# A matrix is loaded in squares of 32 by 32 and turned by VectorE, instead of in rows and turned by TensorE

## The chip, the cores and the metric

The kernel runs on one core of one Trainium2 chip. The metric is the device time of one execution in microseconds (us). The kernel before was timed in three runs: the median is 1117.33 us, the lowest 1117.31, the highest 1117.41. The profile comes from one more execution, taken by the hardware profiler.

A core has five engines that run side by side, each with its own queue of instructions that it takes strictly in order: TensorE (PE in the profile, with its weight loads shown apart as PEld), VectorE (DVE), ScalarE (ACT), GpSimd (POOL) and SyncE (SP). SP, ACT and POOL can also issue DMA transfers. PE reads SBUF and writes PSUM.

## The reference, cut to what matters

The network has two layers of feed-forward block, mixer, cross attention and a second feed-forward block, on 256 tokens of width 1024. The change concerns only `mem`, the memory of 256 rows and 1024 columns that cross attention reads:

```
def cross_attn(x, mem, wq, wk, wv, wo):
    ...
    q = (x @ wq).reshape(bsz, s, CA_HEADS, CA_HEAD_DIM)
    k = (mem @ wk).reshape(bsz, m, CA_HEADS, CA_HEAD_DIM)
    v = (mem @ wv).reshape(bsz, m, CA_HEADS, CA_HEAD_DIM)
```

The products with `ca_k` and `ca_v` contract over the 1024 columns of `mem`. PE contracts over partitions, so the kernel needs `mem` turned: columns on partitions, tokens along the row. The turned memory is made once and used by both layers.

## The kernel before, in words

Everything is float32, and a product is made from rounded parts: `split` (lines 60 to 62) takes a tile, lets ACT round it into a high part (line 61) and lets DVE subtract that from the source, which gives the low part (line 62). A product is then three matmuls, high by high, high by low and low by high (`mm_rows`, lines 127 to 130), all recorded on line 103.

Weights stream from HBM through `load` (lines 64 to 91). SP issues DMAs of 1 MB into a ring of three `raw` tiles (line 75); ACT and DVE split each into `whi` and `wlo` tiles, eight of each. SP therefore runs ahead of PE by as many buffers as the rings hold.

A feed-forward block (`ffn`, line 349) works in chunks of 512 hidden columns, numbered c. For each chunk `hidden` (line 440) makes the gate products and then the up products with `mm_cols`; each group of matmuls fills one PSUM tile `acc`, of which there are four, and ACT and DVE empty it (lines 123 and 124) into a tile `sg` or `up`. Tiles of the tag `up` have two buffers. After the hidden columns of chunk c, `both` multiplies earlier chunks with the down weights into PSUM tiles `dn`.

The memory enters in the first feed-forward block of layer 0. At chunk 1, `early` (lines 497 to 499) calls `load_memory` and `small_parameters`. `load_memory` (lines 174 to 183) issues two DMAs on SP, one for each half of the tokens (line 177), behind the last weight load issued so far. At chunk 2, after `hidden` and ahead of `both` (lines 500 to 502), the functions that both returned are called. The one of the memory transposes in sixteen blocks of 128 by 128: `transposed` and `transposed_half` (lines 164 to 172) let PE transpose four blocks into an `acc` tile (line 167), and `split` empties it into `mT`, the turned memory's high and low part. The one of the parameters transposes one tile `rows` (line 236). The first reader of `mT` is `keys` (line 522), after the first feed-forward block.

`small_parameters` (lines 196 to 259) also fills POOL's queue at the start: six DMAs (lines 198 to 205) and 28 mask operations on a tile `mf` (lines 215 and 219), ended by a conversion into `masks` (line 223). After that POOL has only short powers for the normalisations and a few clearing operations.

The order on each engine is set by an automatic scheduler. It takes instructions in the order of the program as their priority, and puts a later one into a gap where it finds its inputs ready. `tc.issue_after(x)` adds that what its block traces on the engine of x comes behind x in that engine's queue. The first matmuls of the kernel (line 391) and the mixer have orders written out by hand, in which the memory has no part.

Of the kernel before, what the change touches and what calls it, by code (L numbers as in the profile page):

```python
# [8 lines left out]
F32 = mybir.dt.float32  # L9
# [8 lines left out]
P = 128  # L18
DEPTH = 2
SEQ = 256  # L20
DM = 1024
DFF = 2816
NT = SEQ // P
# [23 lines left out]
def model(ctx: ExitStack, tc: tile.TileContext, t: dict, out: bass.AP):  # L47
    nc = tc.nc
# [5 lines left out]
    def acc(shape=(P, 2, SEQ), tag="acc"):  # L54
        return ps.tile(list(shape), F32, tag=tag, name=tag)
# [4 lines left out]
    def split(hi, lo, src):  # L60
        nc.scalar.copy(hi, src)  # L61
        nc.vector.tensor_tensor(lo, src, hi.bitcast(F32), op=ALU.subtract)  # L62
# [69 lines left out]
    def tok(i):  # L132
        return slice(i * P, (i + 1) * P)
# [26 lines left out]
    mTh, mTl = mT[:, :, 0, :], mT[:, :, 1, :]  # L160
# [3 lines left out]
    def transposed_half(src, i, j, dh, dl, unit=idn):  # L164
        pt = acc((P, 4, P))
        for k in range(4):
            nc.tensor.transpose(pt[:, k, :], src[:, (4 * j + k) * P : (4 * j + k + 1) * P], unit)  # L167
        split(dh[:, 4 * j : 4 * j + 4, tok(i)], dl[:, 4 * j : 4 * j + 4, tok(i)], pt)

    def transposed(src, i, dh, dl, unit=idn):  # L170
        for j in range(2):
            transposed_half(src, i, j, dh, dl, unit)

    def load_memory(mp):
        m = [mp.tile([P, DM], F32, tag="m", name="m", bufs=2) for _ in range(NT)]
        for i in range(NT):
            nc.sync.dma_start(m[i], t["mem"][0, tok(i), :])

        def later():
            for i in range(NT):  # L180
                transposed(m[i], i, mTh, mTl)

        return later

# [3 lines left out]
    masks = cst.tile([P, 1024], U8, name="masks")[:, 0 : NT * len(LEVELS) * 64].rearrange(  # L188
        "p (b n c) -> p b n c", b=NT, c=64
    )  # L190
# [5 lines left out]
    def small_parameters(op):  # L196
        nc.gpsimd.memset(rows, 0.0)
        nc.gpsimd.dma_start(rows[0:12, :], t["conv_w"].rearrange("l k (j p) -> (l k j) p", p=P))
        nc.gpsimd.dma_start(rows[12:20, :], t["rec_lb"].rearrange("l (h p) -> (l h) p", p=P))
        nc.gpsimd.dma_start(rows[20:28, :], t["rec_norm_g"].rearrange("l (h p) -> (l h) p", p=P))  # L200
        nc.gpsimd.dma_start(rows[28:32, :], t["pool_scale"].rearrange("l (j p) -> (l j) p", p=P))
        nc.gpsimd.memset(wpool, 0.0)
        for g in range(2):
            q = slice(g * 64, g * 64 + 64)
            nc.gpsimd.dma_start(
                wpool[q, :, :, q].rearrange("r l j c -> r (l j) c"),
                t["pool_w"].rearrange("l (j g) r c -> g r (l j) c", g=2)[g],
            )

        mf = op.tile([P, NT, len(LEVELS), 64], F32, name="mf", bufs=1)  # L210
        nc.gpsimd.memset(mf, 1.0)
        for b in range(NT):
            for n, c in enumerate(LEVELS):
                m = mf[:, b, n, :].rearrange("p (a c) -> p a c", c=c)
                nc.gpsimd.affine_select(
                    out=m, in_=m, compare_op=ALU.is_ge, fill=0.0, base=-b * c,
                    pattern=[[-2 * c, 64 // c], [0, c]], channel_multiplier=1,
                )
                nc.gpsimd.affine_select(
                    out=m, in_=m, compare_op=ALU.is_ge, fill=0.0, base=(1 + b) * c - 1,  # L220
                    pattern=[[2 * c, 64 // c], [0, c]], channel_multiplier=-1,
                )
        nc.gpsimd.tensor_copy(masks, mf)

        cnt = op.tile([P, 2, PAD], F32, name="cnt", bufs=1)
        wcol = op.tile([P, 2], F32, name="wcol", bufs=1)
        for g, w in enumerate(WINDOWS):
            nc.gpsimd.memset(wcol[(g % 2) * 64 : (g % 2) * 64 + 64, g // 2 : g // 2 + 1], float(w))
        nc.gpsimd.iota(
            cnt, pattern=[[0, 2], [1, PAD]], base=1, channel_multiplier=0,  # L230
            allow_small_or_imprecise_dtypes=True,
        )

        def later():
            pt = acc((P, P))
            nc.tensor.transpose(pt, rows, idn)
            nc.vector.tensor_copy(prm, pt[:, 0:32])
            for j in range(2):
                nc.vector.tensor_scalar_min(cnt[:, j, :], cnt[:, j, :], wcol[:, j : j + 1])
            nc.vector.reciprocal(invc, cnt)  # L240

            lb = [prm[:, 12:16], prm[:, 16:20]]
            mx = op.tile([P, HEADS], F32, name="mx", bufs=1)
            nc.vector.tensor_tensor(mx, lb[0], lb[1], op=ALU.max)
            e = op.tile([P, DEPTH, HEADS], F32, name="e", bufs=1)
            s = op.tile([P, HEADS], F32, name="s", bufs=1)
            for l in range(DEPTH):
                nc.vector.tensor_tensor(e[:, l, :], lb[l], mx, op=ALU.subtract)
            nc.scalar.activation(e, e, AF.Exp)
            nc.vector.tensor_tensor(s, e[:, 0, :], e[:, 1, :], op=ALU.add)  # L250
            nc.vector.reciprocal(s, s)
            for l in range(DEPTH):
                nc.vector.tensor_tensor(e[:, l, :], e[:, l, :], s, op=ALU.mult)
            nc.vector.tensor_tensor(lbs[:, 0, :], e[:, 0, :], e[:, 0, :], op=ALU.subtract)
            nc.vector.tensor_tensor(s, e[:, 0, :], e[:, 1, :], op=ALU.add)
            nc.vector.tensor_tensor(lbs[:, 1, :], s, e[:, 0, :], op=ALU.subtract)
            nc.vector.tensor_scalar(oml, lbs, -1.0, 1.0, op0=ALU.mult, op1=ALU.add)

        return later


    def ln_params(l, n):
# [259 lines left out]
    def keys(l, c, between={}):  # L522
        w = load(t["ca_k"][l], 0, NK, c * CHUNK, CHUNK)
        for p in range(2):
            o = sm.tile([P, 2, SEQ], F32, tag="sums", name="sums", bufs=1)
            for j in range(2):
                between.get(4 * p + 2 * j, lambda: None)()
                add(o[:, j, :], mm_cols(w, slice((2 * p + j) * P, (2 * p + j + 1) * P), mT))
            d = slice(4 * c + 2 * p, 4 * c + 2 * p + 2)
            split(kTh[:, d, :], kTl[:, d, :], o)  # L530
# [341 lines left out]
            return project_back([slab(a) for a in (0, 2, 4, 6)], 3, gb, 1.0)  # L872


    pend = None
    for l in range(DEPTH):
        pend = ffn(l, "ffn1", 0, pend, early=None if l else lambda op: (load_memory(op), small_parameters(op)))
        keys(l, 0, {6: pend})
        pend = mixer(l, lambda: keys(l, 1))
        pend = attention(l, pend)  # L880
        pend = ffn(l, "ffn2", 3, pend, last=l == DEPTH - 1)
# [27 lines left out]
```

## Time and profile before

| | |
|---|---|
| median of three runs | 1117.33 us |
| the profiled execution | 1118.65 us |
| its span, first to last instruction | 1116.9 us |
| PE matmuls, busy | 1102.9 us (99%), 6227 instructions |
| PE weight loads, busy | 992.6 us (89%) |
| DVE, busy | 822.4 us (74%) |
| ACT, busy | 594.2 us (53%) |
| POOL, busy | 41.8 us (4%) |
| granted TensorE clock, mean | 0.998 |
| DMA, mean over the span | 195 GB/s |

A row of the timeline gives the start of a group of like instructions in us from the span's start, the time from the first's start to the last's end, the engine, the line, the operation, the tile written and the tiles read, and how many there were; a bracket tells how long the engine had been idle before, and what ended that. Matmuls are pipelined, so the end of one lies behind the start of the next: the pace of PE is read from starts, not from durations. A row of waits gives who waited for whom, the total, how often, and the longest. Weight loads run a little ahead of their matmuls.

### The profile page before, as it was taken

The numbers are of one execution on the slowest core, as the hardware profiler recorded it, in microseconds if no ns is written. First come the engines' busy times: TensorE is split into PE (matmuls) and PEld (weight loads), VectorE is DVE, ScalarE is ACT, GpSimd is POOL, SyncE is SP. The second block draws the span as 40 slices with busy tenths as digits, with TensorE's granted clock in tenths as the row PEclk, the third lists the DMA queues.
The fourth block names the chain that finished last, engine by engine and source line by source line (L and its number), as shares of the span: only waits on it lengthen the run. The fifth ranks groups of instructions, "written<-read, shape, count | busy, mean of one in ns | idle before, by whom it ended". The sixth has DMA issues, their size and how long they took to land. (4 is left out here: it accounts for less than half of the span.)

```text
span 1116.9 us, 15747 instructions
## 1 busy us (share of the span) xinstructions
PE 1102.9 (99%) x6227; PEld 992.6 (89%) x6227; DVE 822.4 (74%) x1195; ACT 594.2 (53%) x873; POOL 41.8 (4%) x80
## 2 busy tenths in 40 slices
PE   9999999999999999999999999999999999999997
PEld 7989998998889889999889999889988998999996
DVE  6766677898888666666677666598988777766665
ACT  6665553645466456455355555455454653665550
POOL 7000000000000000000000000000000000000000
PEclk9999999999999999999999999999999999999999
DMA  8855565743465375656466655655445645755551
GB/s 309 301 211 202 194 221 156 240 170 139 163 243 180 105 262 191 226 204 211 151 226 234 214 182 186 237 186 194 151 146 183 237 152 164 249 189 203 181 182 38
DMA packets 98378, 218.23 MB, mean 195 GB/s; under 512 B 3776, under 2 KB 16352, under 8 KB 98304
## 3 DMA queue, kind: packets, MB, share of 16 engines
q1 hardware_dynamic: 97536, 215.89, 56.1%
q8 instruction: 49, 0.80, 0.3%
q10 hardware_dynamic: 576, 1.18, 0.3%
q14 instruction: 25, 0.20, 0.1%
q0 software_dynamic: 192, 0.15, 0.0%
HBM read 216.15 MB, written 1.05 MB: 194 GB/s over the span
## 5 line engine op out<-in xcount | busy, mean ns | idle before, releaser
L62 DVE TENSOR_TENSOR wlo<-raw,whi 128x1024 fp32r<-128x1024 f32 (+1 forms) x396 | 469.1, 1208 | 102.6 <-ACT whi L61 66.6
L61 ACT CAST whi<-raw 128x1024 fp32r<-128x1024 f32 (+1 forms) x396 | 398.2, 1041 | 170.7 <-PE dn L103 127.6
L103 PE MATMUL acc<-xT,whi 128*128 128x512 f32 x1600 | 388.3, 381 | 0.6 <-DVE xT L62 0.6
L103 PEld LDWEIGHTS acc<-xT,whi 128*128 128x128 f32 x1600 | 288.9, 190 | 33.8 <-DVE xT L62 1.1
L103 PEld LDWEIGHTS acc<-xT,wlo 128*128 128x128 f32 x1600 | 209.7, 191 | 10.8
L103 PE MATMUL acc<-xT,wlo 128*128 128x256 f32 x1600 | 210.8, 275 | 0.0
L103 PE MATMUL dn<-whi,ah 128*128 128x512 f32 x346 | 131.6, 380 | 0.0
L103 PE MATMUL dn<-wlo,ah 128*128 128x512 f32 x346 | 131.1, 379 | 0.0
L103 PE MATMUL dn<-whi,al 128*128 128x512 f32 x346 | 131.1, 379 | 0.0
L103 PE MATMUL dn<-whi,xT 128*128 128x512 f32 x288 | 88.9, 384 | 0.0
L103 PE MATMUL acc<-whi,xT 128*128 128x512 f32 x288 | 88.4, 381 | 0.0
L124 DVE TENSOR_TENSOR sg<-acc,sg 128x256 f32<-128x256 f32 x72 | 30.4, 422 | 69.7 <-ACT sg L123 69.6
L103 PEld LDWEIGHTS dn<-whi,al 128*128 128x128 f32 x346 | 65.4, 189 | 9.3
L103 PEld LDWEIGHTS dn<-wlo,ah 128*128 128x128 f32 x346 | 65.4, 189 | 9.2
L103 PEld LDWEIGHTS dn<-whi,ah 128*128 128x128 f32 x346 | 65.5, 189 | 8.6
L123 ACT COPY sg<-acc 128x256 f32<-128x256 f32 x72 | 26.7, 371 | 84.0 <-PE acc L103 83.8
L103 PEld LDWEIGHTS dn<-whi,xT 128*128 128x128 f32 x288 | 54.8, 191 | 7.5
L103 PEld LDWEIGHTS acc<-whi,xT 128*128 128x128 f32 x288 | 54.3, 189 | 7.6
L103 PE MATMUL dn<-wlo,xT 128*128 128x512 f32 x144 | 54.9, 381 | 0.0
L103 PE MATMUL acc<-wlo,xT 128*128 128x512 f32 x144 | 54.6, 379 | 0.0
L123 ACT COPY up<-acc 128x256 f32<-128x256 f32 x72 | 26.7, 370 | 49.0 <-PE acc L103 48.0
L304 POOL TENSOR_TENSOR rs<-rs,nhalf 128x1 f32<-128x1 f32 x16 | 14.9, 933 | 903.6 <-DVE rs L303 903.6
(196 smaller groups left out, 1048.5 us busy)
## 6 DMA issues: line engine op xcount, KB each, us to landing
raw<-in_ffn_up_dram SPq DMA_DIRECT2D x44, 1024.0 KB, 5.1
raw<-in_ffn_down_dram SPq DMA_DIRECT2D x44, 1024.0 KB, 4.9
raw<-in_ffn_gate_dram SPq DMA_DIRECT2D x42, 1024.0 KB, 5.0
raw<-in_w_in_dram SPq DMA_DIRECT2D x24, 1024.0 KB, 5.1
raw<-in_ca_k_dram SPq DMA_DIRECT2D x8, 1024.0 KB, 5.0
raw<-in_w_out_dram SPq DMA_DIRECT2D x8, 1024.0 KB, 4.9
raw<-in_ca_v_dram SPq DMA_DIRECT2D x8, 1024.0 KB, 6.0
raw<-in_ca_q_dram SPq DMA_DIRECT2D x8, 1024.0 KB, 5.0
```

The costliest lines, as they stand in the source:

```text
L61: nc.scalar.copy(hi, src)
L62: nc.vector.tensor_tensor(lo, src, hi.bitcast(F32), op=ALU.subtract)
L103: nc.tensor.matmul(o, w, x, start=start, stop=stop)
L123: nc.scalar.copy(dst, o[:, 1])
L124: nc.vector.tensor_tensor(dst, o[:, 0], dst, op=ALU.add)
L304: nc.gpsimd.tensor_tensor(rs, rs, nhalf[:, 0:1], op=ALU.pow)
```

## The change

`mem` is loaded by 32 DMAs issued on POOL, in place of two on SP. Each moves, for one strip of 32 columns, all 256 tokens into 32 partitions: the partition is the token's place within its group of 32, and along the row lie the eight groups with 32 columns each. So a tile holds squares of 32 by 32, each where it will be wanted, but each not yet turned; a run of consecutive bytes is 32 floats, 128 bytes. The DMAs are put behind the conversion to `masks` in POOL's queue. At chunk 2 four DVE transposes of 128 by 512 turn the squares, each into a tile of the tag `up`, and four `split`s write `mT` from there. The two functions at chunk 2 now come in the other order, the parameters first. PE's sixteen transposes and their four `acc` tiles are gone; the number and the size of the `split`s are the same.

```diff
-    def load_memory(mp):
-        m = [mp.tile([P, DM], F32, tag="m", name="m", bufs=2) for _ in range(NT)]
-        for i in range(NT):
-            nc.sync.dma_start(m[i], t["mem"][0, tok(i), :])
+    def load_memory(mp, behind):
+        m = [mp.tile([P, 4, 8, 32], F32, tag="m", name="m", bufs=2) for _ in range(2)]
+        with tc.issue_after(behind.ins):
+            for n in range(2):
+                for a in range(4):
+                    for k in range(4):
+                        c = (4 * n + k) * P + a * 32
+                        nc.gpsimd.dma_start(
+                            m[n][a * 32 : a * 32 + 32, k],
+                            t["mem"][0, :, c : c + 32].rearrange("(b i) j -> i b j", i=32),
+                        )
 
         def later():
-            for i in range(NT):
-                transposed(m[i], i, mTh, mTl)
+            for n in range(2):
+                for k in range(0, 4, 2):
+                    turned = mp.tile([P, 2, SEQ], F32, tag="up", name="turned")
+                    nc.vector.transpose(
+                        turned.rearrange("p k t -> p (k t)"), m[n][:, k : k + 2].rearrange("p k b j -> p (k b j)")
+                    )
+                    d = slice(4 * n + k, 4 * n + k + 2)
+                    split(mTh[:, d, :], mTl[:, d, :], turned)
...
-        nc.gpsimd.tensor_copy(masks, mf)
+        made = nc.gpsimd.tensor_copy(masks, mf)
...
-        return later
+        return later, made
...
+    def beginnings(op):
+        parameters, made = small_parameters(op)
+        return parameters, load_memory(op, made)
+
     pend = None
     for l in range(DEPTH):
-        pend = ffn(l, "ffn1", 0, pend, early=None if l else lambda op: (load_memory(op), small_parameters(op)))
+        pend = ffn(l, "ffn1", 0, pend, early=None if l else beginnings)
```

## The prediction

> **What bounds the kernel.** I read the page's busy times first, then the waits of PE and its weight loads, then the timeline of PE around the transposes that go.
>
> ```profile
> span 1116.9 us, 15747 instructions
> PE 1102.9 (99%) x6227; PEld 992.6 (89%) x6227; DVE 822.4 (74%) x1195; ACT 594.2 (53%) x873; POOL 41.8 (4%) x80
> ```
>
> PE has 14 us without work in the whole span. In the waits of the first 120 us, nothing behind the first 9 us stops PE or its weight loads but the two idle times at the memory's and the parameters' transposes. So PE sets the end here, and what leaves its queue comes off the time, unless something takes its place. The stage in question, by its timeline:
>
> ```profile
> 78.38 0.38 PE L103 MATMUL acc<-xT,whi 128*128 128x512 f32 x1
> 78.59 1.47 PE L167 MATMUL acc<-idn,m 128*128 128x128 f32 x12
> 79.82 0.46 PE L103 MATMUL dn<-whi,ah 128*128 128x512 f32 x1
> 80.12 0.38 PE L103 MATMUL dn<-wlo,ah 128*128 128x512 f32 x1
> 80.34 0.38 PE L103 MATMUL dn<-whi,al 128*128 128x512 f32 x1
> 80.71 0.66 PE L167 MATMUL acc<-idn,m 128*128 128x128 f32 x4
> 81.35 0.30 PE L236 MATMUL acc<-idn,rows 128*128 128x128 f32 x1
> 81.41 0.46 PE L103 MATMUL dn<-whi,ah 128*128 128x512 f32 x1
> 81.71 0.38 PE L103 MATMUL dn<-wlo,ah 128*128 128x512 f32 x1
> ```
>
> Read the starts: twelve transposes from 78.59 to 79.82 (0.1025 us each), three `dn` products, four more transposes from 80.71, the parameters' `rows`, then products again. A steady product takes 0.215 us (81.71 to the next at 81.92); the first behind transposes takes 0.30 (79.82 to 80.12), so changing kind costs 0.085. The last four transposes also waited for a PSUM tile:
>
> ```profile
> PEld acc L167 <- DVE up L124: 0.4, 1, 0.4
> ```
>
> **What PE saves.** From 78.595 (78.38 + 0.215) to 81.71 is 3.115 us. Four products remain in it, 4 x 0.215 = 0.86; this leaves 2.255. `rows` stays: its transpose 0.1025 and one change of kind 0.085, together 0.19, and 0.20 more if the weight load's idle time ahead of it ("issue" in the waits) stays. So PE saves 2.255 - 0.19 = 2.07 at most and 2.255 - 0.39 = 1.87 at least. From the other side: sixteen transposes 1.64, one change of kind 0.085, the wait for PSUM on the matmul's side 0.155 (80.34 + 0.215 to 80.71), together 1.88. I take 2.0.
>
> **SP.** Its two DMAs of the memory go, 1.23 us of issue from 27.69 to 28.92 in SP's timeline; the down load behind them, issued at 29.02, comes as much earlier. PE uses that load from 52.45, and it landed 10.3 us after its issue, so nobody waits less.
>
> **POOL.** 32 DMAs of 32 KB are added behind the conversion to masks. The nearest rows are:
>
> ```profile
> 4.61 1.30 POOL L205 DMA_DIRECT2D wpool<-in_pool_w_dram x2
> 20.98 1.80 POOL L223 CAST masks<-mf 128x896 uint8<-128x896 f32 x1
> wpool<-in_pool_w_dram POOLq DMA_DIRECT2D x2, 64.0 KB, 5.8
> ```
>
> One `wpool` DMA has 64 partitions of four rows of 256 bytes: 256 rows, as many as a new one has (32 partitions, eight rows of 128 bytes). It holds POOL for 0.654 us and lands 5.8 us after issue. POOL is free at 22.8. So 32 x 0.654 = 20.9 us of issue; the first half of the squares is there at 22.8 + 10.5 + 5.8 = 39.1, the second at 49.5. Below, the `rows` DMAs bound it, 0.52 each: 45.2 for the second half. Above, a row of POOL under load:
>
> ```profile
> L219 POOL TENSOR_SCALAR_AFFINE_SELECT mf<-mf x14: 242/404/1220, 9.2 to 19.7; 128x64 f32<-128x64 f32 x14
> ```
>
> The same mask operation takes 0.242 us or up to 1.220, the long ones between 15.5 and 18.3 us, while DVE runs the subtractions of line 62. The six DMAs were issued before 5.9, when DVE had nothing but one clearing. If issue suffers in the same ratio, 0.654 x 5.0 = 3.3 us each, and 32 take 105 us: the squares would land at 134, behind chunk 2. I take 0.654, the row nearest in kind, and keep the other end for the rival below. POOL's next work is the power of the normalisation, about 100 us later; nothing queues behind the DMAs.
>
> [...]
>
> **DMA.** Bytes are the same, 1.05 MB, but in runs of 128 bytes. The queues of the first 10 us compare sizes:
>
> ```profile
> q1 hardware_dynamic: 1075, 1.97, 55.4%
> q0 software_dynamic: 182, 0.14, 5.0%
> ```
>
> Of 160 engine-us, SP's queue used 88.6 for 1.97 MB, 45 us per MB; POOL's, mostly rows of 256 bytes, 8.0 for 0.14 MB, 57. So the new loads take between 47 engine-us (as long rows do) and, if the cost of a run is all fixed, 120 (twice 57): 3.0 to 7.5 us on 16 engines against 3.0 before. I take 3.7 (57 per MB). The DMAs were full from 30 to 40 us (share over 1.0 in the windows) but idle for most of 50 to 55 (0.19). The tightest weights there, chunk 1's up, were split by 36.4 and are used from 41.8 on, their later low parts not before 43.9: 7.5 us of cover. Added delay is 4.5 at most, so nothing; without cover it would cost up to 4.5.
>
> [...]
>
> **DVE and ACT.** Four transposes are added. The trace has none; rows of the same 128x512 take 0.68 (the subtraction into `mT`) and a pass of 128x1024 takes 1.21. Below, 128x256 took 0.42. I take 0.68: 2.7 us more on DVE, range 1.7 to 4.8. The splits stay four, from SBUF instead of PSUM (ACT 0.62 against 0.61). DVE is nearly full from 80 to 90 us, but the weights of the running `dn` products were split by 72.4, and the low parts of chunk 3's gate, made by 86.7, are first used at 92.7: 6.0 us of cover against 2.7 more on DVE and PE 2.0 earlier. `keys` reads `mT` at 185.7. So DVE costs nothing if it is not made to wait, and up to 2.7 if its cover is gone.
>
> **The sum.** The profiled execution is 1118.65 (span 1116.9), 1.32 above the median. 1118.65 - 2.0 = 1116.65; against the median 1117.33 - 2.0 = 1115.3. PE waits for no other engine from there to 190 us, and the waits in the mixer follow from products PE made, so they move along.
>
> **Rivals.**
>
> (a) *DVE stands in its queue for the squares* (slower). A transpose in DVE's order ahead of its data stops everything behind it. That later work is put forward into gaps is seen: line 239, of chunk 2, ran at 8.89 us. The two `up` buffers are unused until 44.9. If the first transpose stands ahead of the subtraction and sum at 34.8 to 35.3, DVE is held until 39.1 + 0.7; PE wants that sum's PSUM tile at 36.65. The tile would be free at about 40.2: PE loses 3.5, net +1.5, 1118.8. At 0.9 us a DMA the squares land at 43, PE loses 7.5: 1122.8. At 2.2 times 0.654 (the mask row's mean, 0.505 over 0.242 is 2.1) they land at 51: about 1131. It decides as soon as PE's loss passes 2.0, that is, squares later than about 37.6 with a transpose queued that early. Against it: between 38 and 50 the same PSUM tiles have 4 to 6 us of cover, and a transpose queued at 75 waits for nothing.
>
> (b) *Given back later*: PE and its weight loads wait about 4 us in the mixer at 260 to 280 us. If those waits hang on something that does not move, the 2.0 go there: 1117.3.
>
> (c) *The short runs slow the weights*: if a run of 128 bytes took the DMA engines as long as one of 512, as the `rows` loads have, the time per byte would be four times that of long rows, 12 us instead of 3.0. Chunk 1's up would be 9 late, 1.5 more than its cover: 1115.3 + 1.5 = 1116.8; with no cover, 1124.3. Against it: 256 bytes cost 27% more, not twice as much.
>
> (d) *More is saved*: all 2.255 and something of the freed PSUM tiles, 1114.8.
>
> **Chances.** Forecast 0.52, (a) 0.26, (b) 0.10, (c) 0.05, (d) 0.07. The bound of 0.2% (about what a measurement of this kernel can tell from no change) is 2.23 us, so the forecast lies just inside "within". Faster: (d) and 0.13 of the forecast, 0.20. Within: 0.39 of the forecast, (b), 0.05 of (a), 0.02 of (c), 0.56. Slower: 0.21 of (a), 0.03 of (c), 0.24. The range goes from 1114.6, (d) with little beyond, to 1123, (a) at 0.9 us a DMA; the forecast alone would be 1114.9 to 1115.6.
>
> **What would show it.** PE should go from the last `acc` product to `dn` products at 0.215 without transposes of `m`. POOL should show 32 DMAs of about 0.65 us from 22.8. DVE should show four transposes of about 0.68, with no wait for a DMA before them. A DVE wait on `m` before 50 us, followed by PE waiting for a sum of line 124, shows (a); ACT waits for `raw` much above 4.7 us in the first 120 show (c).

## The result and the profile after

The changed kernel takes 1115.25 us, the median of 16 runs (1114.99 to 1116.53); the kernel before took 1117.38 beside it, also 16 runs (1117.28 to 1117.67). The ratio is 0.9982, with a 95% interval of 0.9975 to 0.9988: 2.13 us less, 0.18%, just inside the 0.2% that the prediction counts as "within". The forecast was 1115.3, a gain of 2.0. The profiled executions differ by nearly the same, 2.12: 1118.65 before, 1116.53 after. Both lie 1.3 above their medians, so their timelines run about 1.3 us later than those of most experiments below.

The head of the page of the changed kernel:

```profile
span 1114.8 us, 15761 instructions
PE 1100.7 (99%) x6211; PEld 990.6 (89%) x6211; DVE 824.0 (74%) x1199; ACT 593.4 (53%) x873; POOL 60.1 (5%) x112
```

PE has 16 instructions fewer and 2.2 us less work, and the span is 2.1 shorter: all that left PE's queue came off the end. DVE has four more and POOL 32 more, 18.3 us of work that nobody paid for. PE's timeline where the transposes were:

```profile
78.25 0.38 PE L103 MATMUL acc<-xT,whi 128*128 128x512 f32 x1
78.46 0.27 PE L251 MATMUL acc<-idn,rows 128*128 128x128 f32 x1
78.49 0.46 PE L103 MATMUL dn<-whi,ah 128*128 128x512 f32 x1
78.79 0.38 PE L103 MATMUL dn<-wlo,ah 128*128 128x512 f32 x1
...
79.44 0.38 PE L103 MATMUL dn<-wlo,ah 128*128 128x512 f32 x1
```

Take the last `acc` product and the fifth `dn` product behind it: 78.25 and 79.44, 1.19 us, where the kernel before shows 78.38 and 81.71, 3.33. The difference is 2.14. Behind `rows` the products run at their 0.215 again, and nothing of it is given back: the waits in the mixer are the same as before and stand 2.3 us earlier (274.03 against 276.30 for the largest; 0.13 of that is there ahead of the transposes already). The new work in the view of the tile `m` (durations in ns, smallest, median, largest; then first and last start):

```profile
L183 POOL DMA_DIRECT2D m<-in_mem_dram x32: 582/582/638, 22.6 to 46.9; - x32
L192 DVE STREAM_TRANSPOSE turned<-m x4: 704/707/707, 76.3 to 83.2; 128x512 f32<-128x512 f32 x4
its engine sat idle before it (us, times) until:
  DMA m<-in_mem_dram: 6.2, 7
...
DMA to landing us min/median/max: 3.5/6.7/7.4
```

The first transpose of DVE comes at 76.3 us, when the last square has long been there (46.9 and up to 7.4 us to landing, about 54). The idle time listed is POOL's own.

### The profile page after: what moved, and what is told of

It is laid out like the page before. It is cut to its first block, busy times and chain, and to the rows that moved or that the text cites. A ratio compares the mean times of both kernels' runs of the same rounds, so it can differ in the third digit from the quotient of the medians.

```text
span 1114.8 us, 15761 instructions
## 1 busy us (share of the span) xinstructions
PE 1100.7 (99%) x6211; PEld 990.6 (89%) x6211; DVE 824.0 (74%) x1199; ACT 593.4 (53%) x873; POOL 60.1 (5%) x112
## 3 DMA queue, kind: packets, MB, share of 16 engines
HBM read 216.15 MB, written 1.05 MB: 195 GB/s over the span
```

## The experiments

Each kernel ran beside the kernel before on the same chip; ratios are to that kernel, with their 95% interval. The theory is the prediction's: PE's queue alone sets the end here, and the loads, POOL and DVE have cover. The rivals are that the gain comes from the new order (parameters first), that part of it is eaten by short runs or by DVE, and that DVE could be caught in its queue.

### Is it PE's queue alone?

`e1_swap`: the kernel before, with only the order of the two functions at chunk 2 changed.

```diff
-        pend = ffn(l, "ffn1", 0, pend, early=None if l else lambda op: (load_memory(op), small_parameters(op)))
+        pend = ffn(l, "ffn1", 0, pend, early=None if l else lambda op: (load_memory(op), small_parameters(op))[::-1])
```

> The kernel before with one edit: at chunk 2 the parameters come ahead of the memory, as in the changed kernel; rows, TensorE's sixteen transposes and SP's two loads stay. Theory (the gain is the sixteen transposes leaving TensorE's queue): at most 0.3 us of the 2.1 comes from the order, since only the 0.2 us of idle weight load ahead of rows and one change of kind can go; 1117.1 to 1117.4. Rival (the order is what frees the time): 1115.3 to 1116.3.

Measured 1117.16, ratio 0.9998 (0.9989 to 1.0007). The order is worth 0.2 us, which this measurement cannot tell from nothing; on PE's timeline it is 0.18: from the last `acc` product (77.07) to the fifth `dn` product (80.22) 3.15 us, against 3.33.

`e4_half`: columns 0 to 511 come in squares and are turned by DVE, columns 512 to 1023 in rows, with eight transposes on PE. This is the changed kernel's `later` with, for the second half,

```diff
+            for i in range(NT):
+                pt = acc((P, 4, P))
+                for k in range(4):
+                    nc.tensor.transpose(pt[:, k, :], r[i][:, k * P : (k + 1) * P], idn)
+                split(mTh[:, 4:8, tok(i)], mTl[:, 4:8, tok(i)], pt)
```

> Half of the change: columns 0 to 511 of the memory come as squares and are turned by VectorE, columns 512 to 1023 come in rows and are turned by TensorE in eight transposes. Theory: half of 16 x 0.1025 goes, 0.82, and of the changes of kind and the wait for PSUM part; 1116.1 to 1116.5. Rival (the wait for a PSUM tile or the mere presence of transposes is what costs): all or nothing, 1115.3 or 1117.3.

Measured 1116.13, ratio 0.9989 (0.998 to 0.9997): 1.23 saved where the whole change saves 2.12 to 2.13. Its timeline on PE:

```profile
77.34 1.04 PE L195 MATMUL acc<-idn,mr 128*128 128x128 f32 x8
78.13 0.46 PE L103 MATMUL dn<-whi,ah 128*128 128x512 f32 x1
```

From 77.34 to 78.13, the eight that stay take 0.79 us, 0.1 each. From the last `acc` product (77.01) to the fifth `dn` product (79.08) PE takes 2.07 us, 0.88 more than the 1.19 of the changed kernel, and that is what this kernel is behind (1116.13 - 1115.25 = 0.88). The gain goes with the transposes: the 1.23 that this kernel has is the other half and the order's 0.2.

`e2_rows_copy`: the changed kernel with `m` loaded in rows on SP and copied by DVE; it leaves the turning out.

```diff
...
-                        nc.gpsimd.dma_start(
-                            m[n][a * 32 : a * 32 + 32, k],
-                            t["mem"][0, :, c : c + 32].rearrange("(b i) j -> i b j", i=32),
-                        )
...
+            nc.sync.dma_start(m[n].rearrange("p k b j -> p (k b j)"), t["mem"][0, tok(n), :])
...
-                    nc.vector.transpose(
+                    nc.vector.tensor_copy(
```

> The changed kernel with the memory loaded as before, in rows by two DMAs on SP, and a VectorE copy in place of each VectorE transpose, into the same tiles; the memory is not turned at all. Theory: TensorE's queue is the same as in the changed kernel, so the time is too, 1115.1 to 1115.4, whatever queue the memory comes on. Rival (moving the loads from SP to GpSimd is worth something, or the small runs cost something): over 1115.7 or under 1114.8.

Measured 1115.24, ratio 0.9981 (0.9972 to 0.9989), the changed kernel's own time. With long rows and no turning nothing more is gained, so the squares and POOL's 32 DMAs cost nothing that can be seen, and neither do DVE's transposes (0.707 us each in the changed kernel) against the copies that stand in their place here.

### Do the short loads or DVE's extra work cost anything?

`e5_extra_loads`: the kernel before, with the 32 square loads added behind the masks into a tile that nobody reads.

```diff
+        with tc.issue_after(behind.ins):
+            for n in range(4):
+                for a in range(4):
+                    for k in range(2):
+                        c = (2 * n + k) * P + a * 32
+                        nc.gpsimd.dma_start(
+                            m[a * 32 : a * 32 + 32, k],
+                            t["mem"][0, :, c : c + 32].rearrange("(b i) j -> i b j", i=32),
+                        )
```

> The kernel before plus the 32 loads of squares on GpSimd's queue behind the conversion to masks, into a tile that nobody reads; TensorE still turns the rows that SP loads. Theory (the weights have cover): 1117.3 to 1117.6 although the DMA queues carry both loads. Rival (c) (short runs slow the weights): 1118 to 1124.

Measured 1117.45 beside 1117.30, ratio 1.0002 (0.9993 to 1.0011). The loads alone cost nothing that can be measured.

`e3_turn_twice`: the changed kernel, each DVE transpose done twice, 2.8 us more on DVE.

```diff
+                    for _ in range(2):
                         nc.vector.transpose(
```

> The changed kernel with each of the four VectorE transposes done twice into the same tile, so 2.8 us more on VectorE in the stage. Theory (VectorE has cover there): no change, 1115.1 to 1115.4. Rival (VectorE's turns already eat part of the gain): 1115.6 to 1118, up to 2.8 more.

Measured 1115.28, ratio 0.9981 (0.9973 to 0.999). DVE's cover holds for twice the added work.

### Rival (a): can DVE be caught in its queue?

`e9_own_tag`: the turned tile no longer shares the two buffers of the tag `up`; it has one of its own, free from the start.

```diff
-                    turned = mp.tile([P, 2, SEQ], F32, tag="up", name="turned")
+                    turned = mp.tile([P, 2, SEQ], F32, tag="turned", name="turned", bufs=1)
```

> The changed kernel with the turned squares in a buffer of their own (one) instead of the two that they share with the up sums. Nothing else is edited; the scheduler can now put the transposes forward, and in VectorE's queue the first stands behind chunk 0's sixth large subtraction, at about 26 us. Rival (a) of the prediction (VectorE stands in its queue for squares that are still on their way): held from 26 to about 38 us, the subtractions behind it are wanted by TensorE from 28 on, and again for the second half; TensorE loses 10 to 17 us: 1125 to 1132. Theory without (a) (wherever they stand, the turns are hidden): 1115.3.

Measured 1127.41, ratio 1.0091 (1.0076 to 1.0107): 12.2 us more than the changed kernel. Three lines tell it, one of DVE's timeline and one of PE's (the bracket is the idle time before it), and one of the waits:

```profile
37.21 0.71 DVE L192 STREAM_TRANSPOSE turned<-m 128x512 f32<-128x512 f32 x1 [11.67 <-DMA m<-in_mem_dram]
```

```profile
39.08 0.80 PE L103 MATMUL acc<-xT,wlo 128*128 128x256 f32 x2 [6.82 <-DVE wlo L62]
```

```profile
PE acc L103 <- DVE wlo L62: 7.2, 2, 6.8
PE acc L103 <- DVE sg L124: 1.4, 1, 1.4
```

The scheduler put the first transpose forward into DVE's queue; DVE stood 11.67 us for the squares, and the subtractions behind it, which make PE's low weights, came late. This is rival (a). PE's waits are 7.2 and 1.4, 8.6. About 2.3 more is the clock, which had fallen: from the first `acc<-xT,whi` product to the transposes of `sg` PE takes 14.70 us (30.15 to 44.85), where the changed kernel takes 5.24 (30.49 to 35.73), 9.46 more with 7.2 of waits. The changed kernel's profile runs 1.3 late, so its 30.49 is about 29.2 here; the 1.0 that this kernel is behind at 30.15 already was lost ahead of the waits, and its cause is open. Together that is 11.9 of the 12.2. The clock (a window of two us: busy time of PE, PEld, DVE, ACT and POOL, then the granted clock, the DMA share and GB/s):

```profile
38.00:40.00 2.00, 0.80 (x2) 0.50 (x2) 2.00 (x2) 2.00 (x3) 2.00 (x4) 0.50 0.30 61
```

`e11_own_tag_held` tells place from buffer: the same own tile, but the transposes are put behind chunk 2's last product of gate and up in DVE's queue.

```diff
+                    with tc.issue_after(ends[-1].ins):
+                        nc.vector.transpose(
...
-                    nc.vector.tensor_tensor(s, r, s, op=ALU.mult)
+                    ends.append(nc.vector.tensor_tensor(s, r, s, op=ALU.mult))
```

> The kernel e9_own_tag (turned squares in one buffer of their own) with one edit: the transposes stand behind the last product of gate and up of chunk 2 in VectorE's queue, by issue_after. Theory (e9 lost its time to the place of the transposes in the queue): 1115.1 to 1115.5. Rival (the own buffer, one instead of two, costs it): 1125 to 1128 as e9.

Measured 1115.33, ratio 0.9982 (0.9973 to 0.9991), with the transposes from 81.2 to 91.8 us. So it was the place in the queue and not the buffer. In the changed kernel the shared tag `up` keeps that place late.

`e6_early`: the changed kernel with the memory's function called at chunk 1, between the two: early, but behind the squares.

```diff
-                if c == 2:
-                    for f in rest:
-                        f()
+                if c == 1 and rest:
+                    rest[1]()
+                if c == 2 and rest:
+                    rest[0]()
```

> The changed kernel with the memory's part called at chunk 1 instead of chunk 2, so that the transposes stand in VectorE's queue from about 53 us on, behind the sums of chunk 1, where the last squares land at about 54. Theory: the first half of the squares is there by 40, the second half at most 1 to 2 us late, which TensorE's cover there (4 to 6 us) takes: 1115.1 to 1115.5. Rival (any transposes ahead of chunk 2 cost as in e9): 1117 or more.

Measured 1115.33, ratio 0.9983 (0.9973 to 0.9992). The transposes ran from 50.3 to 57.9 us, and PE waited for none of it.

### Which queue issues the loads

`e7_sp`: the changed kernel with the 32 loads issued on SP.

```diff
-                        nc.gpsimd.dma_start(
+                        nc.sync.dma_start(
```

> The changed kernel with its 32 loads issued on SP instead of GpSimd, at the place in SP's queue where the two old loads stood. Theory: each holds SP for about 0.6 us as the old ones did, 19 us in all, so the gate weights of chunk 2 land some 15 us later, near 58 to 60 us, when TensorE wants them from 57.5 on: 1116 to 1122, with TensorE waiting in 55 to 75 us. Rival (SP has cover for all of it): 1115.3.

Measured 1122.0 (1121.2 to 1122.62), ratio 1.0041 (1.0027 to 1.0055). SP's timeline, then PE's:

```profile
27.16 19.56 SPq L183 DMA_DIRECT2D m<-in_mem_dram  x32
46.82 0.40 SPq L75 DMA_DIRECT2D raw<-in_ffn_down_dram  x1
```

```profile
54.49 1.22 PE L103 MATMUL dn<-whi,ah 128*128 128x512 f32 x2 [3.24 <-ACT whi L61]
...
56.33 0.63 PE L103 MATMUL dn<-whi,al 128*128 128x512 f32 x1
56.76 0.63 PE L103 MATMUL dn<-wlo,ah 128*128 128x512 f32 x1
```

The 32 issues hold SP for 19.56 us, 0.61 each, and the down load, next in the queue, is issued at 46.82 instead of 28.34. I had expected the gate load behind it, at 57.5, to be the first that is late; it was the down load, at 50.9. PE waited 3.24 and then ran at half its pace, 0.43 from start to start (56.33 to 56.76), until 60.17: 12 products in 5.68 us where they take 2.58, 3.1 more. Together 6.3 of the 6.75 lost against the changed kernel. The loads are the same as with POOL; that SP's queue has the weights behind them makes the difference.

### Taking the parameters' transpose away too

`e8_params_dve`: `rows` also comes in strips, by sixteen DMAs on POOL behind the masks, and DVE turns it into `prm`.

```diff
-            pt = acc((P, P))
-            nc.tensor.transpose(pt, rows, idn)
-            nc.vector.tensor_copy(prm, pt[:, 0:32])
+            nc.vector.transpose(prm, rows)
```

> The changed kernel with the same method for the parameters: rows comes in strips of 32 columns by sixteen small loads on GpSimd, behind the conversion to masks and ahead of the squares, and VectorE turns it; TensorE's last transpose in the stage goes. Theory: the five products behind the last sum took 1.19 us with rows in front, 1.08 without, so 0.11 less: 1115.1 to 1115.2. Rival (the sixteen more loads delay the squares past their use, or cost nothing and gain nothing): 1115.3 or more.

Measured 1123.33 (1122.5 to 1124.16), ratio 1.0053 (1.0041 to 1.0066). This was a miss by 8 us. DVE's timeline and PE's:

```profile
14.35 0.39 DVE L259 TENSOR_SCALAR cnt<-cnt,wcol 128x16 f32<-128x16 f32 x2 [5.42 <-POOL cnt L251]
```

```profile
15.72 1.22 PE L103 MATMUL dn<-whi,xT 128*128 128x512 f32 x2 [5.17 <-DVE xT L62]
```

In this kernel, where the early `rows` DMAs are gone, POOL's filling of `cnt` (IOTA in its timeline) stands at 14.15 us instead of 7.28, behind most of the mask operations; why the scheduler put it there is not shown. DVE's operation on `cnt`, put forward as before, stood 5.42 us at the head of DVE's queue, and with it the subtraction that PE needs. PE waited 5.17, and the eight products behind the wait took 3.31 us (15.72 to 19.03) instead of 1.72, 1.6 more: 6.8 of the 8.1 lost. It is rival (a) again, with another tile and POOL in place of a DMA.

`e10_params_held` takes that out: `cnt` is made first on POOL, and the turned `rows` goes through a tile of the tag `up`, then a copy (the edit is shown against `e8_params_dve`).

```diff
+        nc.gpsimd.iota(
+            cnt, pattern=[[0, 2], [1, PAD]], base=1, channel_multiplier=0,
+            allow_small_or_imprecise_dtypes=True,
+        )
...
-            nc.vector.transpose(prm, rows)
+            turned = op.tile([P, 2, SEQ], F32, tag="up", name="turned")
+            nc.vector.transpose(turned[:, 0, 0:32], rows)
+            nc.vector.tensor_copy(prm, turned[:, 0, 0:32])
```

> The kernel e8_params_dve with its two early waits taken away: GpSimd makes cnt ahead of the masks again, so that the sum of line 239 that VectorE has put forward finds it, and VectorE turns rows into a tile of the tag up and copies it from there, so that this turn stands behind the sums of chunk 2 too. Theory (TensorE's queue sets the end; e8 lost its time to VectorE standing for cnt): 1115.0 to 1115.25, 0.11 less than the changed kernel. Rival (the sixteen small loads or the work on VectorE cost something themselves): 1116 to 1123.

Measured 1115.74 (1115.58 to 1116.86), ratio 0.9987 (0.9978 to 0.9996): the 7.6 us of `e8_params_dve` are back, but it is 0.5 behind the changed kernel, not level or ahead. PE's queue did lose `rows`: the last `acc` product starts at 76.79 and the first `dn` product 0.22 behind it. The span isn't longer either: its median is 1113.5 us over the eleven runs, as over the sixteen of the changed kernel, so the 0.11 does not show there. What grew lies outside the span: 2.0 to 3.6 us in these runs, 2.2 in the median, where the changed kernel has 1.7 to 1.8. The profiled execution is the worst of them (1116.86 with 1113.3 of span). In the span the DMA queue that the page calls q8, kind "instruction", has 48 packets in this kernel and 49 in the changed one; whether another comes behind the span's end and makes the time is not shown. The cause of the 0.5 is open.

## Why the prediction was right

**PE sets the end: right, and shown.** Eight transposes are worth 0.88 and the whole change 2.13, and `e2_rows_copy`, which takes PE's part away but loads in rows on SP and only copies on DVE, gives the same 1115.24.

**The size: 2.0 forecast, 2.14 in PE's timeline, 2.13 in the medians.** The term that was off is `rows`. I left it 0.19 to 0.39. Alone in front it takes 0.11: from 78.25 + 0.215 to 78.49 is 0.025, and the first `dn` product behind it is 0.085 longer (78.49 to 78.79). Hence 2.255 - 0.11 = 2.14, past the 2.07 that I had called the most. The 0.2 of idle weight load ahead of `rows`, which I had left open, is gone, and by the order: in `e1_swap`, too, `rows` takes 0.11 in front (77.29 to 77.40), while the wait of 0.4 for PSUM remains there.

**SP: nobody waits less, right.** But the down load behind the two DMAs that went came only 0.7 us earlier, at 28.34 instead of 29.02, not the whole 1.23.

**POOL: no cost, right, with two sizes off.** One issue took 0.58, not 0.654. But I had left out that POOL waits for its own loads: its timeline shows eight, then seven, then between one and seven at a time. It begins:

```profile
22.59 4.66 POOL L183 DMA_DIRECT2D m<-in_mem_dram  x8
28.01 4.02 POOL L183 DMA_DIRECT2D m<-in_mem_dram  x7 [0.76 <-DMA m<-in_mem_dram]
33.99 0.58 POOL L183 DMA_DIRECT2D m<-in_mem_dram  x1 [1.96 <-DMA m<-in_mem_dram]
```

So the last square landed at about 54 instead of 49.5. With the transposes at 76 this cost nothing; the bound of 3.3 us an issue fell. DVE spent about 6.2 of the 10 us from 30 to 40 on subtractions of line 62, the issues there took 0.58 to 0.59, and the slowest of all 32 took 0.638, at 22.6, so these subtractions did not hold the issues up.

**DMA: no cost, right; its price was far too low, and its cover held.** From 25 to 50 us SP's queue moved 6.22 MB and POOL's 0.98; in the kernel before, SP's moved 8.62, the memory included, in the same stretch (columns: packets, MB, share of 16 engines; after, then before):

```profile
q1 hardware_dynamic: 2638, 6.22, 86.5%
q0 software_dynamic: 952, 0.98, 15.6%
```

```profile
q1 hardware_dynamic: 3602, 8.62, 93.2%
```

Of 25 x 16 = 400 engine-us, the squares used 62.4 for 0.98 MB, 64 us per MB (I took 57), and SP's loads 346 for 6.22 MB, 55.6 per MB, where they used 43.2 per MB before (373 for 8.62) and I had 45. I counted the delay of the squares alone; the weights beside them became slower too. At 43.2 SP's loads would have used 269. If the 77 more are put on the squares, an estimate, their price is 139 engine-us for 0.98 MB, 142 per MB, above the 120 for 1.05 MB that I had as the most. The two loads of chunk 2's gate landed 12.8 us after their issue (median) instead of 8.1: 4.7 more, where I had put the added delay at 4.5 at most. In the window 30 to 40 us the same share of busy DMA time (1.03) moved 309 GB/s instead of 397:

```profile
30.00:40.00 10.00, 10.00 (x64) 9.17 (x63) 7.61 (x11) 4.70 (x8) 6.63 (x12) 1.00 1.03 309
```

The idle stretch from 50 to 55 filled up, from a share of 0.19 and 73 GB/s to 1.00 and 317. It shows in ACT's waits of the first 120 us, where this one had been 4.7 before:

```profile
ACT whi L61 <- DMA raw<-in_ffn_up_dram: 10.3, 4, 4.0
```

Two more, 2.2 each for the gate and the down weights, had been missing before. Together that is 10 us more of ACT waiting for `raw`, the sign that I had named for rival (c): waits much above 4.7. The sign came, the cost did not: PE's waits from 10 to 300 us are the same three in both kernels (1.2, 0.6 and 0.2), and `e5_extra_loads` has the loads with no gain and no loss. So the sign was ill chosen: the wait on ACT showed delay, and only a wait on PE would have shown cost.

**DVE: no cost, right.** A transpose of 128x512 takes 0.707 us, where I took 0.68 from a range of 0.42 to 1.21. Twice as many cost nothing either.

**Rivals.** (a) is real as a mechanism and did not happen: 76.3 us is where the first transpose stood, as in the case "queued at 75". I gave it 0.26 because I couldn't tell where the scheduler would put it, so that it came out late was a chance taken and not worked out; what decides is that `turned` needs a buffer of `up`, which chunk 2 also uses. `e9_own_tag` shows what it costs without that, 1127.4, inside the 1118.8 to 1131 of the prediction, though PE waited mainly for low weights (6.8) and less for the sum of line 124 (1.4), which the prediction had named alone, and part of the price was the clock. (b) fell: the mixer's waits of before stand there with the same totals. (c) fell as a cost, but not as a price: the estimate of 142 against 43.2 engine-us per MB is 3.3 times, near the four times that it assumed, and the cover took it. That a run of 128 bytes takes as long as one of 512, which the four times rested on, no run shows. (d) is close to what came in PE's timeline, 2.14 of the 2.255, but PSUM's release gave nothing beyond it.

## What to carry to other kernels

Work that leaves the queue of the engine that sets the end came off the time one for one here, 0.88 for half and 2.13 for all of the transposes, because what replaced it stood in queues with cover; read the gain from starts on that engine, since transposes have a change of kind with them (0.085 us here, 79.82 to 80.12 before against the steady 0.215). What turned such a change into a loss, in `e9_own_tag` and `e8_params_dve`, was not the added work but the place of one instruction in an in-order queue, ahead of its data (DVE stood 11.67 and 5.42 us): tie it behind something late, by a shared buffer or an explicit order, if its data come late. Many small loads belong on a queue with nothing behind them: 32 issues of about 0.6 us cost nothing on POOL and 6.75 us on SP.

## What was not expected of the hardware

- **Three long waits cost PE more than their length.** After PE had stood for 3.24 us (`e7_sp`), 5.17 (`e8_params_dve`) or 6.82 (`e9_own_tag`), the granted clock stood at 0.50, and products came at 0.43 instead of 0.215. Behind the wait that cost another 3.1, 1.6 and about 2.3 us, so it is no fixed share of the wait. A wait of 1.39 us in `e9_own_tag` left the clock at 1.00. Two windows of `e7_sp`:

```profile
58.00:60.00 2.00, 2.00 (x6) 1.59 (x5) 2.00 (x2) 1.49 (x2) 0.00 (x0) 0.50 0.87 263
60.00:62.00 2.00, 2.00 (x10) 1.69 (x10) 1.37 (x2) 0.10 (x1) 0.00 (x0) 0.93 1.05 407
```

  PE is busy throughout from 58 to 60, yet has 6 matmuls in these two us, and 10 from 60 to 62. Worked out from the means of such windows, the half lasted 6.8 us in `e7_sp`, 3.4 in `e8_params_dve` and 6.8 in `e9_own_tag`. In `e7_sp` the clock fell at 53.4, 2.2 us after PE's last product ended, and was back at 60.3, 5.8 us after work began. What sets these times is not shown. The prediction priced rival (a) by its waits alone.
- **POOL never had more than eight of its square loads under way** in the changed kernel, counted from issue to landing, and stood 6.2 us, in 7 waits, for its own. Whether eight is a limit is not shown.
- **The squares made the loads beside them dear**: 55.6 engine-us per MB for SP's loads, instead of 43.2 in the same stretch before. Whether the short runs do it or the second queue is open, since no run loads long rows on POOL.
- **The squares cost more DMA time on SP's queue than on POOL's.** On POOL's queue 0.98 MB, some 7600 runs of 128 bytes, went in 952 packets, 1.03 KB or eight runs each in the mean, and took 64 engine-us per MB. On SP's, in the window 40 to 45 us of `e7_sp`, where SP issues nothing else, the DMA share is 0.36 at 57 GB/s: 28.8 engine-us for 0.285 MB, about 101 per MB, an estimate that puts the whole share on the squares.
- **Time outside the span can grow**: `e10_params_held`, above, 2.0 to 3.6 us against 1.7 to 1.8; open.
